# The end of a down-projection: gain rows fetched one stage earlier, factors by square root and reciprocal, the third row tile finished ahead of the fourth

## The chip, the cores and the metric

One core of one Trainium2 chip runs the kernel. The metric is the device time of one execution in microseconds (us). Smaller is better. Engines: PE (TensorE, the matrix engine), DVE (VectorE), ACT (ScalarE), POOL (GpSimd) and SP (SyncE, which here only issues DMAs).

## The reference, cut to what matters

One layer of an encoder trunk over 512 tokens of width 2048: a token mixer, a cross-attention and a ConvFFN, each with a residual add, and one final RMSNorm. The change lies in the last product and that norm:

```python
def conv_ffn(h, w_up, conv_w, w_down):
    u = causal_dwconv(h @ w_up, conv_w)
    gate, up = u[..., :D_FF], u[..., D_FF:]
    return (jax.nn.silu(gate) * up) @ w_down
...
    x = x + conv_ffn(h, w_ffn_up[l], ffn_conv[l], w_ffn_down[l])
    return rmsnorm(x, final_norm)
```

`rmsnorm` divides each token's row by the root of its mean square plus 1e-6 and multiplies by a gain row of 2048 numbers. D_FF is 5632.

## The kernel before, in words

Float32 products are made of three products of rounded parts: an operand is split into a high and a low part (`hi` by a cast on ACT, `lo` by a subtraction on DVE), and PE adds hi·hi, lo·hi and hi·lo (lines 1214, 1215 and 1216, always in this order).

The down-projection follows a scheme with seven block products in place of eight. It is run as four stages, `ph` 0 to 3 in the code, each with 22 steps `k` (KD = 22). In stages 0 to 2 a step has two halves, `j` 0 and 1, with a weight piece of 128x1024 each, and 12 matmuls of 128x128x512 per half. Stage 3 has one half per step. The list `slots` holds all halves in order. The stationary operand is the hidden activation: `hid` (128x512, loaded from `hf_d` by `fac_load`, line 950, five steps ahead), split by `fac_split` (line 956) one step ahead into `hdh` (ACT, line 149) and `hdl` (DVE, line 150). In stage 3 one `hid` serves two steps. The moving operand is the weight piece: loaded into `wst` (SP, line 854), in half of the cases added to a stored block (DVE, line 1006), and split by `make`/`sum_parts` into `whi` (ACT, line 972) and `wlo` (DVE, line 975), two halves ahead. `whi`, `wlo` have three buffers each, `wst` five.

The order on PE, DVE, ACT and POOL is the order of the code (a manual schedule). The loop over the slots does for each: `fac_load`, `fac_split`, `make`, then one entry of the list `later`, then the matmuls (`rows`). The list `later` holds work that has no weight to wait for: each stage's end fills it, and one entry leaves it per slot from step 1 on.

All tiles of 128x512 outside PSUM come from one pool (line 73, 64 buffers, taken by `T`, line 96). A tile gets a buffer that is free, and where none is, its first writer waits for the last reader of the tile that had it. In stage 2 (the third) the following hold buffers from its first step to its last: `store` for the steps up to 17 (line 988, two tiles each, 36), and the quadruples `c12`, `p7`, `c11` and `u2` (16). What is left serves `hid`, `hdh` and `hdl`.

At the end of stage 2 the fifth product gives two of the four row tiles of tokens their final sums (`c11`, `c12`); stage 3 adds the seventh product to the other two (`p7`; `u2` is already complete). The norm is done in stage 3 through `later`: squares on ACT with row sums (line 1222), gain rows from memory to all partitions (four POOL DMAs, `gains`, line 1294), the factors of row tiles 0 and 1 (`factor`: row sum, mean, then `rsqrt`, line 227 on, as the exponential of a logarithm on ACT with one refinement on DVE), then `out_tile` (line 1231: DVE multiplies by factor and gain, SP stores), and the product of `u2` with its gain (line 1308). The last two steps of stage 3 are held back and run quarter by quarter (lines 1313 to 1315), so that the sums of `p7` (line 1316) start while PE still works; then one `factor` for row tiles 2 and 3, four `out_tile` and four scaled copies on ACT (line 1323), all stored by SP.

Of the kernel before, what the change touches and what calls it, by code (L numbers as in the profile page):

```python
# [9 lines left out]
F32 = mybir.dt.float32  # L10
F32R = mybir.dt.float32r
AF = mybir.ActivationFunctionType
ALU = mybir.AluOpType
AX = mybir.AxisListType

P = 128
S = 512
D = 2048
# [8 lines left out]
EPS = 1e-6  # L27
# [42 lines left out]
def trunk(ctx: ExitStack, tc: tile.TileContext, g):  # L70
    nc = tc.nc
# [3 lines left out]
    sp = ctx.enter_context(tc.tile_pool(name="sp", bufs=2))  # L75
# [16 lines left out]
    def nm(s):  # L92
        uid[0] += 1
        return f"{s}_{uid[0]}"

    def T(s, dt=F32):
        return tp.tile([P, S], dt, tag="t", name=nm(s))
# [30 lines left out]
    cst = cpool.tile([P, 4], F32, tag="cst", name="cst")  # L128
# [116 lines left out]
    def rstd(ps, ms):  # L245
        nc.vector.tensor_scalar(ms, ps, 1.0 / D, EPS, op0=ALU.mult, op1=ALU.add)
        return rsqrt(ms, ps, 1.0 / D, cst[:, 0:1])
# [144 lines left out]
    for step in range(2 * KT):  # L392

        i, q = ((0, 0), (1, 0), (0, 1), (1, 1))[step] if step < 4 else divmod(step, 2)
# [309 lines left out]
    for i in range(8):  # L704
        for t in (1, 2, 0):
# [5 lines left out]
            elif t == 2:  # L711
                nc.vector.tensor_tensor(cg, ps, cg, op=ALU.mult)
                y = T("ysc")
# [56 lines left out]
    for half in range(2):  # L770
        for gq in range(2):
# [15 lines left out]
            for tq in range(2):  # L787
                j = 2 * half + tq
# [61 lines left out]
    tt = nc.vector.tensor_tensor  # L850
# [50 lines left out]
    with tc.manual_schedule(engines={mybir.EngineType.PE}):  # L901
        for idx in range(KT):
            n = order2[idx]
# [26 lines left out]
    def US(t):  # L930
        return us[0].tile([P, 1024], F32, tag="us", name=nm(t))
# [15 lines left out]
    def fkey(ph, k):  # L947
        return (ph, k // 2 * 2) if ph == 3 else (ph, k)
# [137 lines left out]
    for i in range(NF):  # L1086
# [27 lines left out]
        if i:  # L1114
            s2 = US("s2")
            tt(s2, s1, a11, op=ALU.subtract)
        else:
            s2 = a11
# [56 lines left out]
    def conv_step(c, a=0):  # L1175
        if not a:
            cv = T("ucv")
            tail.append(cv)
            nc.scalar.activation(cv, tail[-2], AF.Identity, scale=col(c + 2))
            a = 1  # L1180
        nc.vector.scalar_tensor_tensor(tail[-1][:, a:], tail[-2][:, : S - a], col(c + 2 - a), tail[-1][:, a:], op0=ALU.mult, op1=ALU.add)

    def gated():
# [6 lines left out]
    later = [gate_sum, lambda: conv_step(C_FCONV + 3 * last_i), lambda: conv_step(C_FCONV + 3 * last_i, 2), gated, up_sum,  # L1190
             lambda: conv_step(C_FCONV + 3 * (NF + last_i)), lambda: conv_step(C_FCONV + 3 * (NF + last_i), 2),
             lambda: tt(tail[1], tail[1], tail[3], op=ALU.mult)]
# [11 lines left out]
    def rows(bs, w, xs, off, first, last, only=None):  # L1204
        hi, lo = w
        xh, xl = xs
        for b in range(4) if only is None else (only,):
            t, ns = b // 2, b % 2
            c = slice(off + t * P, off + (t + 1) * P)
            n = slice(ns * S, (ns + 1) * S)  # L1210
            mm3_(bs[b], xh[:, c], xl[:, c], hi[:, n], lo[:, n], first, last)
# [6 lines left out]
    def add_rest(dst, j, m):  # L1218
        nc.gpsimd.dma_start(dst, x2t_d[j, :, m * S : (m + 1) * S], accum_op=ALU.add)

    def square(dst, ss, m):
        nc.scalar.activation(PG("sq"), dst, AF.Square, accum_out=ss[:, m : m + 1])

    def factor(ss, s2):

        tot = sp.tile([P, 2], F32, tag="tot", name=nm("tot"))
        nc.vector.tensor_reduce(tot, ss.rearrange("p (j m) -> p j m", j=2), axis=AX.X, op=ALU.add)
        ms = sp.tile([P, 2], F32, tag="ms2", name=nm("ms2"))
        return rstd(tot, ms)

    def out_tile(src, j, m, r):
        o = T("o")
        nc.vector.scalar_tensor_tensor(o, src, r[:, j % 2 : j % 2 + 1], gain[m], op0=ALU.mult, op1=ALU.mult)
        nc.sync.dma_start(g["out"][j][:, m * S : (m + 1) * S], o)

    with tc.manual_schedule(engines={mybir.EngineType.Activation, mybir.EngineType.DVE, mybir.EngineType.Pool, mybir.EngineType.PE}):
        for i, (ph, k, j) in enumerate(slots):
            if k == 0 and j == 0:
                bs = [banks(q) for q in range(1 if ph == 3 else 2)]
            a = ph * KD + k  # L1240
            for dist, act in ((5, fac_load), (2 if ph == 3 else 1, fac_split)):
                if a + dist < 4 * KD:
                    act((a + dist) // KD, (a + dist) % KD)
            make(i + 2)
            if ph == 3 and k % 2 == 0:
                add_block()
            if later and k > 0:
                later.pop(0)()
            if ph == 3 and k == KD - 2:
                continue  # L1250
            if ph == 3 and k == KD - 1:
                break
            rows(bs[j], pieces.pop(i), fac[fkey(ph, k)], (k % 2 if ph == 3 else 1 - j if ph == 2 else j) * S2, k == 0, k == KD - 1)
            if k < KD - 1:
                continue
            if ph == 0 and j == 0:
                c12 = quad("c12")
                for c, b in zip(c12, bs[0]):
                    nc.scalar.copy(c, b)
            elif ph == 0:  # L1260
                p7 = quad("p7")
                for c, b in zip(p7, bs[1]):
                    nc.scalar.copy(c, b)
                for q in range(4):
                    later.append(lambda q=q: add_rest(c12[q], q // 2, 2 + q % 2))
            elif ph == 1 and j == 0:
                c11 = quad("c11")
                for c, b in zip(c11, bs[0]):
                    nc.scalar.copy(c, b)
            elif ph == 1:  # L1270
                u2 = quad("u2")
                for u, c, b in zip(u2, c11, bs[1]):
                    tt(u, c, b, op=ALU.add)
                for q in range(4):
                    later.append(lambda q=q: tt(c12[q], c12[q], u2[q], op=ALU.add))
                    later.append(lambda q=q: tt(p7[q], p7[q], u2[q], op=ALU.add))
                for q in range(4):
                    later.append(lambda q=q: add_rest(c11[q], q // 2, q % 2))
            elif ph == 2 and j == 0:
                for q in range(4):  # L1280
                    tt(c11[q], c11[q], bs[0][q], op=ALU.add)
            elif ph == 2:
                ss01 = sp.tile([P, 8], F32, tag="ss01", name="ss01")
                ss23 = sp.tile([P, 8], F32, tag="ss23", name="ss23")
                gain, r, p5 = [], [], bs[1]

                def with_p5(q):
                    tt(u2[q], p7[q], p5[q], op=ALU.add)
                    add_rest(u2[q], 2 + q // 2, 2 + q % 2)
                    add_rest(p7[q], 2 + q // 2, q % 2)  # L1290
                    tt(c12[q], c12[q], p5[q], op=ALU.add)
                    square(c11[q], ss01, q // 2 * 4 + q % 2)

                def gains():
                    for m in range(4):
                        gain.append(T("gain"))
                        nc.gpsimd.dma_start(gain[m], g["fin"][:, m * S : (m + 1) * S].broadcast_to([P, S]))

                for q in range(4):
                    later.append(lambda q=q: with_p5(q))  # L1300
                for q in range(4):
                    later.append(lambda q=q: square(c12[q], ss01, q // 2 * 4 + 2 + q % 2))
                later.append(gains)
                later.append(lambda: r.append(factor(ss01, "a")))
                for q in range(4):
                    later.append(lambda q=q: (out_tile(c11[q], q // 2, q % 2, r[0]), square(u2[q], ss23, q // 2 * 4 + 2 + q % 2)))
                for q in range(4):
                    later.append(lambda q=q: (out_tile(c12[q], q // 2, 2 + q % 2, r[0]), tt(u2[q], u2[q], gain[2 + q % 2], op=ALU.mult)))
        for run in later:
            run()  # L1310
        nc.scalar.activation(cst[:, 3:4], cst[:, 0:1], AF.Ln)
        n = len(slots)
        for q in range(4):
            for i in (n - 2, n - 1):
                rows(bs[0], pieces[i], fac[fkey(3, KD - 2)], (i - n + 2) * S2, False, i == n - 1, only=q)
            tt(p7[q], p7[q], bs[0][q], op=ALU.add)
            square(p7[q], ss23, q // 2 * 4 + q % 2)
        rb = factor(ss23, "b")
        for q in range(4):
            j, m = 2 + q // 2, q % 2  # L1320
            out_tile(p7[q], j, m, rb)
            o = T("o")
            nc.scalar.activation(o, u2[q], AF.Identity, scale=rb[:, q // 2 : q // 2 + 1])
            nc.sync.dma_start(g["out"][j][:, (2 + m) * S : (3 + m) * S], o)


# [55 lines left out]
```

## Time and profile before

| | |
|---|---|
| three timed runs | 2753.11, 2755.22 and 2755.49 us; median 2755.22 |
| profiled execution, span from its first to its last instruction | 2753.7 us |
| PE busy | 2721.7 us (99%) |
| DVE, ACT, POOL busy | 2099.9, 1426.7, 267.5 us |
| mean granted PE clock | 0.997 |
| DMA, mean | 174 GB/s |

The page gives the span of the profiled execution as its own time; the timed runs are others. A row of the timeline reads: start in us from the span's start, duration in us (of the whole group where several are merged, "x2"), engine, line, operation, written tile <- read tiles, shape; in brackets the idle time of the engine ahead of it and what ended that. "SPq" is a DMA issue of SP. A busy PE says little by itself, since matmuls overlap: 0.39 us is one matmul's time from start to end, and what counts is the distance between starts.

### The profile page before, as it was taken

The numbers are of one execution on the slowest core, as the hardware profiler recorded it, in microseconds if no ns is written. First come the engines' busy times: TensorE is split into PE (matmuls) and PEld (weight loads), VectorE is DVE, ScalarE is ACT, GpSimd is POOL, SyncE is SP. The second block draws the span as 40 slices with busy tenths as digits, with TensorE's granted clock in tenths as the row PEclk, the third lists the DMA queues.
The fourth block names the chain that finished last, engine by engine and source line by source line (L and its number), as shares of the span: only waits on it lengthen the run. The fifth ranks groups of instructions, "written<-read, shape, count | busy, mean of one in ns | idle before, by whom it ended". The sixth has DMA issues, their size and how long they took to land.

```text
span 2753.7 us, 38057 instructions
## 1 busy us (share of the span) xinstructions
PE 2721.7 (99%) x14045; PEld 2300.9 (84%) x14045; DVE 2099.9 (76%) x3335; ACT 1426.7 (52%) x2092; POOL 267.5 (10%) x258
## 2 busy tenths in 40 slices
PE   9999999999999999999999999999999999999997
PEld 8888878888788888888788888888888888888885
DVE  7777647878775324445679999999999999877877
ACT  6674644345443323324566655556565655455455
POOL 2120001012110000110020000000000000000201
PEclk9999999999999999999999999999999999999999
DMA  7786853333332234445566677766767676864976
GB/s 266 236 294 195 270 174 105 109 95 93 107 92 90 90 102 139 147 149 169 168 174 178 172 191 185 188 182 182 194 180 189 176 195 202 257 186 146 290 229 177
DMA packets 213931, 479.35 MB, mean 174 GB/s; under 512 B 26720, under 2 KB 94192, under 8 KB 213744
## 3 DMA queue, kind: packets, MB, share of 16 engines
q1 hardware_dynamic: 154688, 372.81, 41.8%
q0 software_dynamic: 20272, 62.94, 12.8%
q10 hardware_dynamic: 38784, 41.17, 4.3%
q8 instruction: 110, 1.80, 0.3%
q14 instruction: 77, 0.63, 0.1%
HBM read 424.13 MB, written 52.71 MB: 173 GB/s over the span
## 4 chain that ended last, share of the span: by engine, by line
PE 67%; DVE 2%; DMA 1%; issue 1%; ACT 0%; DVEq 0%; SPq 0%; ACTq 0%
PE px L169 11%; PE px L172 6%; PE pz L169 6%; PE psd L1216 4%; PE psd L1215 4%; PE psd L1214 4%; PE psx L155 3%; PE pssc L154 3%; PE psx L154 3%; PE psx L156 3%; PE pssc L156 3%; PE pssc L155 3%; PE pz L172 3%; PE py L169 3%; PE py L172 1%; PE pss L781 1%
## 5 line engine op out<-in xcount | busy, mean ns | idle before, releaser
L144 DVE TENSOR_TENSOR wlo<-wst,whi 128x1024 fp32r<-128x1024 f32 x316 | 392.8, 1244 | 283.2 <-ACT whi L143 281.3
L143 ACT CAST whi<-wst 128x1024 fp32r<-128x1024 f32 x316 | 331.7, 1050 | 513.4 <-PE pssc L155 134.9
L169 PE MATMUL px<-xo,whi 128*128 128x512 f32 x1408 | 354.9, 394 | 4.5 <-ACT gb L1121 1.9
L860 ACT CAST whi<-wst 128x1024 fp32r<-128x1024 f32 x177 | 186.0, 1051 | 217.2 <-PE pz L169 126.5
L169 PEld LDWEIGHTS px<-xo,whi 128*128 128x128 f32 x1408 | 254.2, 189 | 51.2 <-ACT gb L1121 2.1
L1216 PE MATMUL psd<-wlo,hdh 128*128 128x512 f32 x616 | 240.6, 391 | 5.2 <-DVE wlo L975 5.2
L1215 PE MATMUL psd<-whi,hdl 128*128 128x512 f32 x616 | 239.8, 389 | 0.9 <-DVE hdl L150 0.9
L1214 PE MATMUL psd<-whi,hdh 128*128 128x512 f32 x616 | 239.8, 389 | 0.1
L861 DVE TENSOR_TENSOR wlo<-wst,whi 128x1024 fp32r<-128x1024 f32 x177 | 215.0, 1215 | 1.7 <-ACT whi L860 1.7
L172 PEld LDWEIGHTS px<-xo,wlo 128*128 128x128 f32 x1408 | 192.4, 191 | 13.8
L172 PE MATMUL px<-xo,wlo 128*128 128x256 f32 x1408 | 196.5, 282 | 0.0
L169 PE MATMUL pz<-xo,whi 128*128 128x512 f32 x704 | 176.3, 392 | 0.0
L860 ACT CAST whi<-s 128x1024 fp32r<-128x1024 f32 x131 | 136.2, 1040 | 76.1 <-PE px L169 38.7
L972 ACT CAST whi<-wst 128x1024 fp32r<-128x1024 f32 x99 | 104.3, 1053 | 122.1 <-issue 60.5
L861 DVE TENSOR_TENSOR wlo<-s,whi 128x1024 fp32r<-128x1024 f32 x131 | 159.3, 1216 | 0.0
L154 PE MATMUL psq<-hh,whi 128*128 128x512 f32 x384 | 156.0, 406 | 0.0
L154 PE MATMUL pssc<-hh,whi 128*128 128x512 f32 x384 | 153.2, 399 | 0.0
L156 PE MATMUL psq<-hh,wlo 128*128 128x512 f32 x384 | 150.6, 392 | 0.0
L155 PE MATMUL psq<-hl,whi 128*128 128x512 f32 x384 | 150.3, 391 | 0.0
L156 PE MATMUL pssc<-hh,wlo 128*128 128x512 f32 x384 | 149.9, 390 | 0.0
L155 PE MATMUL pssc<-hl,whi 128*128 128x512 f32 x384 | 149.6, 390 | 0.0
L169 PEld LDWEIGHTS pz<-xo,whi 128*128 128x128 f32 x704 | 126.6, 189 | 22.6
(362 smaller groups left out, 5924.5 us busy)
## 6 DMA issues: line engine op xcount, KB each, us to landing
wst<-in_w_up SPq DMA_DIRECT2D x132, 512.0 KB, 3.9
wst<-in_w_dn SPq DMA_DIRECT2D x121, 512.0 KB, 4.5
wst<-in_w_mix SPq DMA_DIRECT2D x112, 512.0 KB, 3.5
s<-in_w_up POOLq DMA_DIRECT2D x87, 512.0 KB, 6.1
s<-in_w_up SPq DMA_DIRECT2D x43, 512.0 KB, 4.4
hid<-hf_d SPq DMA_DIRECT2D x77, 256.0 KB, 5.3
wst<-in_w_xq SPq DMA_DIRECT2D x32, 512.0 KB, 5.1
wst<-in_w_xv SPq DMA_DIRECT2D x32, 512.0 KB, 3.6
```

The lines of the kernel that those rows point to most:

```text
L143: nc.scalar.copy(hi, st)
L144: nc.vector.tensor_tensor(lo, st, f(hi), op=ALU.subtract)
L154: nc.tensor.matmul(ps, wh, xh, start=first, stop=False)
L155: nc.tensor.matmul(ps, wh, xl, start=False, stop=False)
L156: nc.tensor.matmul(ps, wl, xh, start=False, stop=last)
L169: nc.tensor.matmul(ps, hi[:, k * P : (k + 1) * P], x, start=first and k == 0, stop=False, skip_group_check=True)
L172: nc.tensor.matmul(ps[:, n:], lo[:, k * P : (k + 1) * P], x[:, :n], start=False, stop=end, skip_group_check=True)
L860: nc.scalar.copy(hi, t)
L861: nc.vector.tensor_tensor(lo, t, f(hi), op=ALU.subtract)
L1214: nc.tensor.matmul(ps, xh, wh, start=first, stop=False)
L1215: nc.tensor.matmul(ps, xl, wh, start=False, stop=False)
L1216: nc.tensor.matmul(ps, xh, wl, start=False, stop=last)
```

## The change

Four things change. The gain rows are fetched by an entry of `later` that the end of stage 1 adds, so in stage 2, behind the thirteenth slot of it, and not in stage 3. `factor` takes the square root on ACT and the reciprocal on DVE, with the same refinement, and the early load of the logarithm's table is gone. Row tiles 2 and 3 get separate factors: row tile 2 is summed, scaled and stored while row tile 3's sums follow. The last two scaled copies are stored through ACT's own DMA queue. (As `later` in stage 3 is one entry shorter, each entry behind the gains leaves it one slot sooner.)

```diff
-    def factor(ss, s2):
+    def total(ss, n):
 
-        tot = sp.tile([P, 2], F32, tag="tot", name=nm("tot"))
-        nc.vector.tensor_reduce(tot, ss.rearrange("p (j m) -> p j m", j=2), axis=AX.X, op=ALU.add)
-        ms = sp.tile([P, 2], F32, tag="ms2", name=nm("ms2"))
-        return rstd(tot, ms)
+        tot, ms, y = (sp.tile([P, n], F32, tag=f"fa{n}{s2}", name=nm(s2)) for s2 in ("tot", "ms2", "fy"))
+        nc.vector.tensor_reduce(tot, ss.rearrange("p (j m) -> p j m", j=n), axis=AX.X, op=ALU.add)
+        nc.scalar.activation(y, tot, AF.Sqrt, scale=1.0 / D, bias=cst[:, 0:1])
+        nc.vector.tensor_scalar(ms, tot, 1.0 / D, EPS, op0=ALU.mult, op1=ALU.add)
+        return ms, y
+
+    def refined(ms, y):
+
+        t = sp.tile([P, ms.shape[1]], F32, tag=f"fa{ms.shape[1]}ft", name=nm("ft"))
+        nc.vector.reciprocal(y, y)
+        nc.vector.tensor_tensor(t, y, y, op=ALU.mult)
+        nc.vector.scalar_tensor_tensor(t, t, -0.5, ms, op0=ALU.mult, op1=ALU.mult)
+        nc.vector.scalar_tensor_tensor(y, t, 1.5, y, op0=ALU.add, op1=ALU.mult)
+        return y
+
+    def factor(ss, n):
+
+        return refined(*total(ss, n))
...
                 for q in range(4):
                     later.append(lambda q=q: add_rest(c11[q], q // 2, q % 2))
+                gain = []
+
+                def gains():
+                    for m in range(4):
+                        gain.append(T("gain"))
+                        nc.gpsimd.dma_start(gain[m], g["fin"][:, m * S : (m + 1) * S].broadcast_to([P, S]))
+
+                later.append(gains)
...
-                later.append(gains)
-                later.append(lambda: r.append(factor(ss01, "a")))
+                later.append(lambda: r.append(factor(ss01, 2)))
...
-        nc.scalar.activation(cst[:, 3:4], cst[:, 0:1], AF.Ln)
...
-            tt(p7[q], p7[q], bs[0][q], op=ALU.add)
-            square(p7[q], ss23, q // 2 * 4 + q % 2)
-        rb = factor(ss23, "b")
-        for q in range(4):
-            j, m = 2 + q // 2, q % 2
-            out_tile(p7[q], j, m, rb)
-            o = T("o")
-            nc.scalar.activation(o, u2[q], AF.Identity, scale=rb[:, q // 2 : q // 2 + 1])
-            nc.sync.dma_start(g["out"][j][:, (2 + m) * S : (3 + m) * S], o)
...
+        def last_scaled(q, r, queue):
+            o = T("o")
+            nc.scalar.activation(o, u2[q], AF.Identity, scale=r)
+            queue.dma_start(g["out"][2 + q // 2][:, (2 + q % 2) * S : (3 + q % 2) * S], o)
+
+        for q in range(4):
+            last_rows(q)
+        for q in range(2):
+            last_sum(q)
+            square(p7[q], ss23, q)
+        half = total(ss23[:, 0:4], 1)
+        last_sum(2)
+        square(p7[2], ss23, 4)
+        ra = refined(*half)
+        out_tile(p7[0], 2, 0, ra)
+        last_sum(3)
+        for q in range(2):
+            last_scaled(q, ra, nc.sync)
+        square(p7[3], ss23, 5)
+        out_tile(p7[1], 2, 1, ra)
+        rb = factor(ss23[:, 4:8], 1)
+        for q in (2, 3):
+            out_tile(p7[q], 3, q % 2, rb)
+            last_scaled(q, rb, nc.scalar)
```

Where instructions stand now, at three places. First DVE in stage 2, the steps 9 and 10, with what each row waits for (PE_49 is the count of matmuls done, Activation_49 that of ACT, DMAHW those of SP's DMAs). Before:

```order
L150 TENSOR_TENSOR hdl_23542<-hid_23353,hdh_23541 128x512 [waits DMAHW2_49,Activation_49]
L1006 TENSOR_TENSOR wst_23545<-wst_23545,store_21493 128x512 [waits DMAHW4_49]
L1006 TENSOR_TENSOR wst_23545<-wst_23545,store_21494 128x512
L975 TENSOR_TENSOR wlo_23550<-wst_23521,whi_23549 128x1024 [waits DMAHW3_49,PE_49,Activation_49]
L975 TENSOR_TENSOR wlo_23568<-wst_23545,whi_23567 128x1024 [waits PE_49,Activation_49]
L150 TENSOR_TENSOR hdl_23586<-hid_23401,hdh_23585 128x512 [waits DMAHW5_49,Activation_49]
```

Now:

```order
L150 TENSOR_TENSOR hdl_23550<-hid_23353,hdh_23549 128x512 [waits DMAHW2_49,PE_49,Activation_49]
L1006 TENSOR_TENSOR wst_23553<-wst_23553,store_21493 128x512 [waits DMAHW4_49]
L1006 TENSOR_TENSOR wst_23553<-wst_23553,store_21494 128x512
L975 TENSOR_TENSOR wlo_23558<-wst_23529,whi_23557 128x1024 [waits DMAHW3_49,Activation_49]
L975 TENSOR_TENSOR wlo_23576<-wst_23553,whi_23575 128x1024 [waits Activation_49]
L150 TENSOR_TENSOR hdl_23594<-hid_23401,hdh_23593 128x512 [waits DMAHW5_49,PE_49,Activation_49]
```

The order is the same; `hdl` has PE among its waits, which `wlo` behind it no longer needs. This holds for each `hdl` of the steps 9 to 18 of stage 2, and the count waited for is that of the last matmul of line 1215 of the step before (for step 10: the last one that reads `hdl` of step 9). Step 19 has no such wait, and 20 and 21 wait for matmuls of two steps before.

Second POOL's DMA issues in stage 2 and at their end in stage 3 (`store` is a block of the weights added to a stored one, `gain` a gain row). Before:

```order
L1024 DMA store_21234<-in_w_dn 128x512
L1024 DMA store_21235<-in_w_dn 128x512
L1024 DMA store_21340<-in_w_dn 128x512
L1024 DMA store_21341<-in_w_dn 128x512
...
L1024 DMA store_22019<-in_w_dn 128x512 x2
L1297 DMA gain_24415<-in_fin 128x512
L1297 DMA gain_24417<-in_fin 128x512
L1297 DMA gain_24419<-in_fin 128x512
L1297 DMA gain_24421<-in_fin 128x512
```

Now:

```order
L1024 DMA store_21234<-in_w_dn 128x512
L1024 DMA store_21235<-in_w_dn 128x512
L1298 DMA gain_23509<-in_fin 128x512
L1298 DMA gain_23511<-in_fin 128x512
L1298 DMA gain_23513<-in_fin 128x512
L1298 DMA gain_23515<-in_fin 128x512
L1024 DMA store_21340<-in_w_dn 128x512
L1024 DMA store_21341<-in_w_dn 128x512
```

The four gain DMAs moved from the end of POOL's queue to a place ahead of the additions to `store` of stage 2.

Third DVE at the end of the program (`p` is `p7`, `o` an output tile, `rsy` and `fy` a factor). Before:

```order
L1316 TENSOR_TENSOR p_3930_22159<-p_3930_22159,psd_24165 128x512
L1316 TENSOR_TENSOR p_3931_22160<-p_3931_22160,psd_24166 128x512
L1227 TENSOR_REDUCE tot_24735<-ss_24162 128x2
L246 TENSOR_SCALAR ms_4442_24737<-tot_24735 128x2
L240 TENSOR_TENSOR rst_24742<-rsy_24739 128x2
L241 SCALAR_TENSOR_TENSOR rst_24742<-rst_24742,ms_4442_24737 128x2
L242 SCALAR_TENSOR_TENSOR rsy_24739<-rst_24742,rsy_24739 128x2
L1233 SCALAR_TENSOR_TENSOR o_24746<-p_3928_22157,rsy_24739,gain_24415 128x512
L1233 SCALAR_TENSOR_TENSOR o_24752<-p_3929_22158,rsy_24739,gain_24417 128x512
```

Now:

```order
L1227 TENSOR_REDUCE tot_24728<-ss_24170 128x1
L1229 TENSOR_SCALAR ms_4440_24729<-tot_24728 128x1
L1334 TENSOR_TENSOR p_3930_22159<-p_3930_22159,psd_24173 128x512
L1235 RECIPROCAL fy_24730<-fy_24730 128x1
L1236 TENSOR_TENSOR ft_24737<-fy_24730 128x1
L1237 SCALAR_TENSOR_TENSOR ft_24737<-ft_24737,ms_4440_24729 128x1
L1238 SCALAR_TENSOR_TENSOR fy_24730<-ft_24737,fy_24730 128x1
L1247 SCALAR_TENSOR_TENSOR o_24742<-p_3928_22157,fy_24730,gain_23509 128x512
L1334 TENSOR_TENSOR p_3931_22160<-p_3931_22160,psd_24174 128x512
L1247 SCALAR_TENSOR_TENSOR o_24754<-p_3929_22158,fy_24730,gain_23511 128x512
L1227 TENSOR_REDUCE tot_24757<-ss_24170 128x1
L1229 TENSOR_SCALAR ms_4450_24758<-tot_24757 128x1
```

The sums of the third and fourth quarter now stand behind the reduction and behind the first factor and output tile of row tile 2.

More of the change, by code (lines that the diff above doesn't have):

```diff
@@ L1222, in square @@
         nc.scalar.activation(PG("sq"), dst, AF.Square, accum_out=ss[:, m : m + 1])
-    def factor(ss, s2):
-        tot = sp.tile([P, 2], F32, tag="tot", name=nm("tot"))
-        nc.vector.tensor_reduce(tot, ss.rearrange("p (j m) -> p j m", j=2), axis=AX.X, op=ALU.add)
-        ms = sp.tile([P, 2], F32, tag="ms2", name=nm("ms2"))
-        return rstd(tot, ms)
+    def total(ss, n):
[13 more added lines that the diff above has]
+        return refined(*total(ss, n))
     def out_tile(src, j, m, r):
         o = T("o")
-        nc.vector.scalar_tensor_tensor(o, src, r[:, j % 2 : j % 2 + 1], gain[m], op0=ALU.mult, op1=ALU.mult)
+        nc.vector.scalar_tensor_tensor(o, src, r, gain[m], op0=ALU.mult, op1=ALU.mult)
         nc.sync.dma_start(g["out"][j][:, m * S : (m + 1) * S], o)
@@ L1284, in trunk @@
                 ss23 = sp.tile([P, 8], F32, tag="ss23", name="ss23")
-                gain, r, p5 = [], [], bs[1]
+                r, p5 = [], bs[1]
                 def with_p5(q):
@@ L1292, in with_p5 @@
                     square(c11[q], ss01, q // 2 * 4 + q % 2)
[L1294 to L1297, printed above, removed]
                 for q in range(4):
@@ L1302, in trunk @@
                     later.append(lambda q=q: square(c12[q], ss01, q // 2 * 4 + 2 + q % 2))
-                later.append(gains)
-                later.append(lambda: r.append(factor(ss01, "a")))
+                later.append(lambda: r.append(factor(ss01, 2)))
                 for q in range(4):
-                    later.append(lambda q=q: (out_tile(c11[q], q // 2, q % 2, r[0]), square(u2[q], ss23, q // 2 * 4 + 2 + q % 2)))
+                    later.append(lambda q=q: (out_tile(c11[q], q // 2, q % 2, r[0][:, q // 2 : q // 2 + 1]), square(u2[q], ss23, q // 2 * 4 + 2 + q % 2)))
@@ L1307, in trunk, with last_rows @@
                 for q in range(4):
-                    later.append(lambda q=q: (out_tile(c12[q], q // 2, 2 + q % 2, r[0]), tt(u2[q], u2[q], gain[2 + q % 2], op=ALU.mult)))
+                    later.append(lambda q=q: (out_tile(c12[q], q // 2, 2 + q % 2, r[0][:, q // 2 : q // 2 + 1]), tt(u2[q], u2[q], gain[2 + q % 2], op=ALU.mult)))
         for run in later:
             run()
-        nc.scalar.activation(cst[:, 3:4], cst[:, 0:1], AF.Ln)
         n = len(slots)
-        for q in range(4):
+        def last_rows(q):
@@ L1314, in trunk, with last_sum @@
             for i in (n - 2, n - 1):
                 rows(bs[0], pieces[i], fac[fkey(3, KD - 2)], (i - n + 2) * S2, False, i == n - 1, only=q)
+        def last_sum(q):
             tt(p7[q], p7[q], bs[0][q], op=ALU.add)
-            square(p7[q], ss23, q // 2 * 4 + q % 2)
-        rb = factor(ss23, "b")
+        def last_scaled(q, r, queue):
+            o = T("o")
+            nc.scalar.activation(o, u2[q], AF.Identity, scale=r)
+            queue.dma_start(g["out"][2 + q // 2][:, (2 + q % 2) * S : (3 + q % 2) * S], o)
```

## The prediction

> **What bounds the kernel now.** I read the page's busy times first, then a table of windows over the last 140 us, then the timelines of DVE, PE, ACT and SP at the places that the change touches. The page:
>
> ```profile
> PE 2721.7 (99%) x14045; PEld 2300.9 (84%) x14045; DVE 2099.9 (76%) x3335; ACT 1426.7 (52%) x2092; POOL 267.5 (10%) x258
> PEclk9999999999999999999999999999999999999999
> ```
>
> PE is busy for 99% of the span, at the full granted clock. An edit can only gain in the few places where PE waits, or behind its last product; it can lose anywhere. The windows (length, then busy time of PE, weight load, DVE, ACT, POOL, then clock, DMA share, GB/s) show where PE waits:
>
> ```profile
> 2600.00:2640.00 40.00, 40.00 (x178) 33.14 (x177) 30.74 (x37) 19.75 (x23) 5.24 (x6) 1.00 0.98 310
> 2640.00:2670.00 30.00, 30.00 (x134) 24.84 (x133) 23.64 (x31) 14.28 (x17) 0.00 (x0) 1.00 0.71 223
> 2710.00:2720.00 10.00, 7.82 (x34) 5.87 (x32) 8.62 (x14) 4.57 (x11) 0.00 (x0) 1.00 0.63 219
> 2720.00:2730.00 10.00, 9.66 (x42) 7.32 (x41) 10.00 (x16) 4.80 (x8) 0.00 (x0) 1.00 0.25 90
> 2730.00:2740.00 10.00, 7.57 (x31) 5.41 (x30) 7.82 (x12) 4.15 (x8) 0.00 (x0) 1.00 0.14 52
> ```
>
> The first two rows lie in stage 2: PE never stops, DVE has a fifth of its time free. The last three lie in stage 3: PE loses time there, and DVE is the busier engine.
>
> **The change part by part.** I begin with the part that decides, the gain rows fetched in stage 2. They take four buffers of the tile pool from the thirteenth slot of stage 2 on. There, 36 buffers hold `store`, 16 the quadruples; of 64 that leaves 12, and with the gain rows 8. Each step keeps five `hid` in flight, and `hdh` and `hdl` of the step on PE: seven. The next `hdh` takes the eighth, so the next `hdl` gets the buffer of the present one, and must wait for the last matmul of line 1215 that reads it, the last but one of the step. The order of DVE, quoted above, shows this wait for ten steps (9 to 18); from then on `hid` is loaded half as often, and a buffer is free.
>
> Queued behind `hdl` on DVE are, for the next step, two additions and both `wlo`; behind the additions ACT's second `whi`; behind these SP's next weight loads and POOL's additions to `store`. PE needs `hdl` for the second product of the step and `wlo` for the third. The rows of DVE for one such chain, and of PE for its pace and for how it follows:
>
> ```profile
> 2661.84 0.69 DVE L150 TENSOR_TENSOR hdl<-hid,hdh 128x512 fp32r<-128x512 f32 x1
> 2662.45 1.29 DVE L1006 TENSOR_TENSOR wst<-wst,store 128x512 f32<-128x512 f32 x2
> 2663.65 1.22 DVE L975 TENSOR_TENSOR wlo<-wst,whi 128x1024 fp32r<-128x1024 f32 x1
> ...
> 2667.28 0.68 DVE L150 TENSOR_TENSOR hdl<-hid,hdh 128x512 fp32r<-128x512 f32 x1
> ```
>
> ```profile
> 2707.67 0.39 PE L1215 MATMUL psd<-whi,hdl 128*128 128x512 f32 x1
> ...
> 2711.53 0.39 PE L1214 MATMUL psd<-whi,hdh 128*128 128x512 f32 x1
> 2712.79 0.50 PE L1215 MATMUL psd<-whi,hdl 128*128 128x512 f32 x1 [0.87 <-DVE hdl L150]
> 2714.59 0.50 PE L1216 MATMUL psd<-wlo,hdh 128*128 128x512 f32 x1 [1.30 <-DVE wlo L975]
> 2714.93 0.39 PE L1214 MATMUL psd<-whi,hdh 128*128 128x512 f32 x1
> ...
> 2740.05 0.39 PE L1216 MATMUL psd<-wlo,hdh 128*128 128x512 f32 x1
> ```
>
> ```profile
> 2712.05 0.68 DVE L150 TENSOR_TENSOR hdl<-hid,hdh 128x512 fp32r<-128x512 f32 x1
> ...
> 2740.47 0.69 DVE L1316 TENSOR_TENSOR p<-p,psd 128x512 f32<-128x512 f32 x1 [0.67 <-PE psd L1216]
> ```
>
> From 2707.67 to 2711.53 are 17 products, so the pitch is 3.86/17 = 0.227 us, and a step of 24 takes 5.45, which is also the distance of the two `hdl` (2667.28 − 2661.84 = 5.44). Call e the end of the matmul waited for. DVE starts on a result of PE about 0.03 after its end (2740.05 + 0.39 = 2740.44; DVE at 2740.47). From the start of `hdl` to the end of the first `wlo` are 2663.65 + 1.22 − 2661.84 = 3.03. PE follows DVE by about 0.06 (2712.05 + 0.68 = 2712.73; PE at 2712.79). So the third product of the next step starts at e + 3.12. Without the wait it would start four pitches after the product that is waited for, at e − 0.39 + 0.91 = e + 0.52. That is a loss of 2.60. After a pause the next product follows by 0.34 in place of 0.227 (2714.59 to 2714.93), which adds 0.11: 2.71 for each step.
>
> The trace of before has one pause of the same form, hung on the same chain: from 2711.53 to 2714.93 three products take 3.40 where three pitches are 0.68, a loss of 2.72. Ten such steps cost 27.1. The bounds of one are 2.5 (if DVE is released one pitch ahead of the modelled end of the matmul) and 3.0 (if PE pays its slow restart twice, for `hdl` and for `wlo`, and 0.50 in place of 0.39 for one of them). DVE cannot make it up ahead: the chain starts only with e, and the next e is a whole step behind.
>
> The Trainium skill ("Perfetto Trace Analysis", "Optimization Strategy") has a rule that speaks against this edit: the same gap repeating on the engine that should be saturated can mean that there is no room for the next tile. Before shows no such gap in stage 2 (PE 40.00 of 40.00); by that rule the changed kernel would show ten.
>
> What the early fetch takes away lies in stage 3, together with the new factor. DVE's rows with the waits, and ACT's beside them:
>
> ```profile
> 2704.74 0.17 DVE L246 TENSOR_SCALAR ms<-tot 128x2 f32<-128x2 f32 x1
> 2706.58 0.16 DVE L240 TENSOR_TENSOR rst<-rsy 128x2 f32<-128x2 f32 x1 [1.68 <-ACT rsy L238]
> ...
> 2707.52 1.23 DVE L975 TENSOR_TENSOR wlo<-wst,whi 128x1024 fp32r<-128x1024 f32 x1 [0.39 <-ACT whi L972]
> ...
> 2711.38 0.75 DVE L1233 SCALAR_TENSOR_TENSOR o<-c,rsy,gain 128x512 f32<-128x512 f32 x1 [2.63 <-DMA gain<-in_fin]
> ```
>
> ```profile
> 2704.74 0.30 ACT L237 ACTIVATE rsy<-tot,cst 128x2 f32<-128x2 f32 x1 [1.51 <-DVE tot L1227]
> 2705.05 1.28 ACT L238 ACT_TABLE_LOAD   x1
> ```
>
> DVE waits 1.68 for the exponential, behind a table load of 1.28, then 0.39 for a `whi` that ACT made late, and 2.63 for the gain rows. With the square root (one ACT operation, as the 0.30 here) DVE waits about 0.16 (2705.04 against 2704.91) if the table stands; the reciprocal adds one small operation, 0.19 with its gap. DVE is the limit here, so 4.70 − 0.16 + 0.19, that is 4.3 of 4.70, should come back. Bounds: 2.6, if only the gain wait goes and a table load stays in the way, and 5.5; not more, since all stops of PE in the stage are 7.0 (from 2711.53 to 2740.05 95 pitches, 21.5, take 28.52), and the first, at 2712.79 and 2714.59, is 2.7 of these.
>
> Behind the last product (2740.44) 13.3 us follow until the span's end at 2753.7. The output tiles on DVE, ACT's work, two of SP's issues, and the time that issues of that line take to land:
>
> ```profile
> 2744.57 2.74 DVE L1233 SCALAR_TENSOR_TENSOR o<-p,rsy,gain 128x512 f32<-128x512 f32 x4
> ```
>
> ```profile
> 2742.46 1.28 ACT L238 ACT_TABLE_LOAD   x1
> ...
> 2744.57 2.56 ACT L1323 ACTIVATE o<-u,rsy 128x512 f32<-128x512 f32 x4 [0.62 <-DVE rsy L242]
> ```
>
> ```profile
> 2745.32 0.33 SPq L1324 DMA_DIRECT2D out_x<-o  x1
> ...
> 2749.18 0.60 SPq L1324 DMA_DIRECT2D out_x<-o  x1
> ```
>
> ```profile
> DMA to landing us min/median/max: 2.2/3.3/3.4
> ```
>
> Before, the factor is ready 4.1 after the last product, eight tiles follow, and SP's eight issues end at 2749.78. Now the table load is gone from that path, but the last sum stands behind the reduction, factor and output tile of row tile 2 and starts about 1.3 later, so the factor of row tile 3 is again ready at about 4.1. Then only two tiles on DVE and two on ACT remain (0.69 and 0.64 each, by the rows of four), with two queues: the last issue starts near 4.1 + 2 × 0.64 + 0.5 = 5.9 in place of 8.74. That is 2.8; with a last landing of 2.2 in place of 3.4, 4.0. I take 3.6, nearer to the second, since the queue before it is shorter.
>
> Then the edits that I cost at nothing: the gain DMAs now stand ahead of twelve additions to `store` in POOL's queue, which are needed only in stage 3. The final weight, its issue, its first reader, and the landing times of that line:
>
> ```profile
> 2701.65 0.34 SPq L854 DMA_DIRECT2D wst<-in_w_dn  x1
> ```
>
> ```profile
> 2730.87 1.28 DVE L1006 TENSOR_TENSOR wst<-wst,store 128x512 f32<-128x512 f32 x2
> ```
>
> ```profile
> DMA to landing us min/median/max: 3.4/6.2/12.4
> ```
>
> The last weight load is issued 29 us ahead of its use, and the slowest landing of the line in the last 210 us took 12.4: sooner buys nothing, and later by 10 would cost nothing.
>
> The sum, on this execution's own span: 2753.7 + 27.1 − 4.3 − 3.6 = 2772.9. The median of the timed runs is 1.5 above that span, so the forecast is 2755.22 + 19.2 = 2774.4.
>
> **The rivals.** First, the other side: the waits stand in the order but do not bite, because `hdl` is let go early enough. That needs the release 2.6 us or more ahead of the end of the step's last product but one, while the reader waited for is that very one. If another buffer is free on the chip all the same (the `hid` of the step gone sooner than the order says), only the gains remain: 2755.2 − 7.9 = 2747.3. It decides from a DVE chain shorter than 0.5 us, against 3.03 in the rows. I give it 0.05.
>
> Second, the clock: PE stops for over 2 us in every step, and its granted clock might fall behind each stop. If the 12 products behind each one ran at half rate, that is 10 × 12 × 0.227 = 27 more: 2801.6. Against it stands the window from 2710 to 2720, clock 1.00 through idle times of 0.87 and 1.30. The Trainium skill ("TensorE: Matmul & The Clock Gate", "Part 1: The HAM clock gate") has the rate halved after an idle window of about 3.4 us; the stops here would be shorter than that, so by that rule the clock stays. Chance 0.03.
>
> Third, the loads: `hid`'s DMA waits for buffers freed later, and SP's weight loads queue behind it. The group of weight loads from 2560 to 2668:
>
> ```profile
> wst<-in_w_dn SPq DMA_DIRECT2D x40, 512.0 KB, 6.3
> ```
>
> A load lands 6.3 after its issue here, at a DMA share of up to 0.98. If the additions had to wait one us more for it in each of the ten steps, the time would be 2784. Against it: slower steps of 8.2 also load the queues less, and five `hid` are in flight. Chance 0.04. That nothing changes at all would need gain and loss to cancel: 7.9 of gain is three stops, not ten; 0.01 with all such mixtures.
>
> **How the numbers follow.** The forecast has 0.87. Its own bounds: ten stops of 2.5 to 3.0 are 25 to 30; the gains 2.6 + 2.8 = 5.4 to 5.5 + 4.0 = 9.5. So +15.5 to +24.6, 2770.7 to 2779.8; one stop more or less that is only half covered widens it to 2769 to 2782. Outside lie the first rival, the second and the third, 0.12 together, so I do not stretch it to them. About 0.2% (5.5 us) is what a measurement of this kernel can tell from no change. Faster by more than that: 0.05; within it: 0.01; slower: 0.94.
>
> **What would show it right or wrong.** In the changed kernel's timeline of DVE, ten `hdl` in stage 2 should start 0.03 behind a PE matmul, one each 8.2 us, and PE should show a pair of stops in each, at `hdl` and at `wlo`, of about 0.3 and 1.8 us; PE's busy share in these 82 us should be about three quarters. In stage 3 the waits of 1.68 and 2.63 should be gone, and the last product should lie about 9.7 from the end. It is wrong if stage 2 shows no stops (first rival), if the clock there is below 1.00 (second), or if DVE's additions wait for `wst` (third).

## The result, and the profile after

The changed kernel takes 2790.06 us (median of 4 runs, 2788.57 to 2790.73), the kernel before 2755.35 beside it. The ratio is 1.0122, 95% interval 1.0111 to 1.0134: slower by 34.7 us, where 19.2 were forecast. The profiled execution spans 2786.8 us, 33.1 more than that of before. The page, its first row and the granted clock:

```profile
PE 2737.7 (98%) x14045; PEld 2306.7 (83%) x14045; DVE 2102.5 (75%) x3343; ACT 1422.2 (51%) x2087; POOL 267.7 (10%) x258
PEclk9999999999999999999999999999999999999999
```

The page hides it: forty slices of 70 us are too coarse for the clock. Two windows in stage 2 show it (columns as before):

```profile
2600.00:2640.00 40.00, 30.17 (x108) 21.77 (x106) 18.81 (x23) 10.07 (x12) 3.49 (x4) 0.91 0.77 211
2640.00:2660.00 20.00, 15.25 (x48) 11.12 (x48) 8.81 (x12) 5.05 (x7) 1.75 (x2) 0.83 0.61 165
```

PE, busy without a break from 2600 to 2670 us before, is now busy for three quarters of the time there, and the granted clock is 0.83 to 0.91. What PE waited for from 2560 us on (total, times, longest):

```profile
PE psd L1216 <- DVE wlo L975: 21.0, 14, 1.8
PE psd L1215 <- DVE hdl L150: 4.2, 10, 0.7
```

Ten stops at `hdl`, as the order said. (Of the fourteen waits for `wlo` ten belong to these stops; the other four are shorter than 0.9 us and lie elsewhere.) The timeline of DVE has the waits on PE in them:

```profile
2601.99 0.69 DVE L150 TENSOR_TENSOR hdl<-hid,hdh 128x512 fp32r<-128x512 f32 x1 [5.86 <-PE psd L1215]
...
2610.23 0.69 DVE L150 TENSOR_TENSOR hdl<-hid,hdh 128x512 fp32r<-128x512 f32 x1 [3.88 <-PE psd L1215]
...
2620.10 0.69 DVE L150 TENSOR_TENSOR hdl<-hid,hdh 128x512 fp32r<-128x512 f32 x1 [5.50 <-PE psd L1215]
...
2628.39 0.69 DVE L150 TENSOR_TENSOR hdl<-hid,hdh 128x512 fp32r<-128x512 f32 x1 [3.93 <-PE psd L1215]
```

The distances are 8.24, 9.87 and 8.29 us: two kinds of steps. PE's timeline shows the difference, one stop of each kind:

```profile
2620.85 0.50 PE L1215 MATMUL psd<-whi,hdl 128*128 128x512 f32 x1 [0.38 <-DVE hdl L150]
2623.19 0.50 PE L1216 MATMUL psd<-wlo,hdh 128*128 128x512 f32 x1 [1.84 <-DVE wlo L975]
2623.53 0.40 PE L1214 MATMUL psd<-whi,hdh 128*128 128x512 f32 x1
...
2631.48 0.67 PE L1216 MATMUL psd<-wlo,hdh 128*128 128x512 f32 x1 [1.84 <-DVE wlo L975]
2631.95 0.63 PE L1214 MATMUL psd<-whi,hdh 128*128 128x512 f32 x1
2632.37 0.63 PE L1215 MATMUL psd<-whi,hdl 128*128 128x512 f32 x1
...
2634.93 0.46 PE L1215 MATMUL psd<-whi,hdl 128*128 128x512 f32 x1
2635.23 0.39 PE L1216 MATMUL psd<-wlo,hdh 128*128 128x512 f32 x1
```

Both have the same pauses (0.4 and 1.84). Behind the first, products follow at full pace; behind the second for 3.45 us at 0.43 in place of 0.227, that is eight products at half rate, 1.6 us more. Such stretches begin behind seven of the ten stops.

Which stops bring the clock down looks like chance, but the trace shows what goes with it. The clock's records have the seven stretches begin at 2614.58, 2631.65, 2641.89, 2652.13, 2662.37, 2679.43 and 2689.68 us. Each lasts 3.41 us, and the distances between the beginnings are 10.24 or 17.07 us, three or five times 3.413. So in this trace the clock changes only at the edges of a fixed grid of 3.413 us. These are the grid windows with the two stops just shown, each with the window behind it (columns as before):

```profile
2621.41:2624.82 3.41, 1.63 (x7) 1.35 (x8) 2.95 (x3) 2.52 (x3) 0.00 (x0) 1.00 0.43 111
2624.82:2628.24 3.42, 3.42 (x17) 2.81 (x16) 0.00 (x0) 0.00 (x0) 0.00 (x0) 1.00 0.74 265
...
2628.24:2631.65 3.41, 1.17 (x5) 0.43 (x4) 3.15 (x5) 1.19 (x2) 1.67 (x2) 1.00 0.36 88
2631.65:2635.06 3.41, 3.41 (x9) 2.63 (x10) 1.11 (x1) 1.32 (x2) 0.08 (x1) 0.50 0.83 136
```

An edge of the grid cuts the first stop, and its window holds 1.78 us without a product (3.41 − 1.63); the clock stays. The second stop lies in one window whole, 2.24 us, and the next window runs at half rate. The ten traces of this document hold 26 such falls ahead of the last product. In 25 of them the window ahead has 1.83 us or more without a product; of the almost 8000 other windows two reach 1.83 (1.83 and 1.84). One fall, in the experiment with three products in the pause, follows a window with 1.52 and stays unexplained. This bound was read off the finished traces; no run was made to try it.

The account by stages needs common points: the sums of `u2` at the beginning of stage 2, those of `c11` behind the first half of its last step, and the last product. Before:

```profile
2551.89 2.48 DVE L1273 TENSOR_TENSOR u<-c,psd 128x512 f32<-128x512 f32 x4
...
2670.29 2.47 DVE L1281 TENSOR_TENSOR c<-c,psd 128x512 f32<-128x512 f32 x4
```

Now:

```profile
2551.62 2.48 DVE L1287 TENSOR_TENSOR u<-c,psd 128x512 f32<-128x512 f32 x4
...
2709.96 2.47 DVE L1303 TENSOR_TENSOR c<-c,psd 128x512 f32<-128x512 f32 x4
```

```profile
2776.21 0.39 PE L1216 MATMUL psd<-wlo,hdh 128*128 128x512 f32 x1
```

| | before | changed | difference | forecast |
|---|---|---|---|---|
| up to stage 2 | 2551.89 | 2551.62 | −0.3 | |
| stage 2 | 118.40 | 158.34 | +39.9 | +27.1 |
| from there to the end of the last product | 70.15 | 66.64 | −3.5 | −4.3 |
| from there to the end | 13.3 | 10.2 | −3.1 | −3.6 |

Stage 2 is ten stops of 8.24 − 5.44 = 2.80 us, 28.0, and seven stretches at half rate of 9.87 − 8.24 = 1.63 us, 11.4: 39.4 of the 39.9. (The tenth stop is 0.35 longer than the others: PE waits 0.74 for `hdl` there in place of 0.39.)

### The profile page after: what moved, and what is told of

Its sections match the earlier page's. It is cut to its first block, busy times and chain, and to the rows that moved or that the text cites. A ratio compares the mean times of both kernels' runs of the same rounds, so it can differ in the third digit from the quotient of the medians.

```text
span 2786.8 us, 38075 instructions
## 1 busy us (share of the span) xinstructions
PE 2737.7 (98%) x14045; PEld 2306.7 (83%) x14045; DVE 2102.5 (75%) x3343; ACT 1422.2 (51%) x2087; POOL 267.7 (10%) x258
## 4 chain that ended last, share of the span: by engine, by line
PE 65%; DVE 3%; DMA 1%; issue 1%; ACT 1%; ACTq 0%; DVEq 0%; SPq 0%
PE px L169 11%; PE px L172 6%; PE pz L169 6%; PE psd L1216 4%; PE psd L1215 4%; PE psd L1214 4%; PE pssc L154 3%; PE pssc L156 3%; PE pssc L155 3%; PE pz L172 3%; PE psx L155 3%; PE psx L154 3%; PE psx L156 3%; PE py L169 3%; PE py L172 1%; PE pss L781 1%
## 5 line engine op out<-in xcount | busy, mean ns | idle before, releaser
L1216 PE MATMUL psd<-wlo,hdh 128*128 128x512 f32 x616 | 246.3, 400 | 21.3 <-DVE wlo L975 21.0
L1215 PE MATMUL psd<-whi,hdl 128*128 128x512 f32 x616 | 245.6, 399 | 4.2 <-DVE hdl L150 4.2
L1216 PEld LDWEIGHTS psd<-wlo,hdh 128*128 128x128 f32 x616 | 118.4, 192 | 52.6 <-DVE wlo L975 28.0
```

What stands on the lines that cost most here:

```text
L1215: nc.tensor.matmul(ps, xl, wh, start=False, stop=False)
L1216: nc.tensor.matmul(ps, xh, wl, start=False, stop=last)
```

## The experiments

My theory after the result: the four buffers of the gain rows make all ten stops, and PE's idle time in a stop, if long enough, brings its clock down. Against it: that the early gain DMAs do harm by themselves (traffic, POOL's queue), that the other parts of the change have a share, or that the low clock has a cause of its own.

### e1_gain_late: the gain rows back in stage 3, the rest of the change kept

```diff
-                later.append(gains)        # end of stage 1
+                later.append(gains)        # end of stage 2, ahead of factor
                 later.append(lambda: r.append(factor(ss01, 2)))
```

> The changed kernel with one part undone: the gain rows are fetched in stage 3 again, the rest of the change stays. If the lack of buffers makes the ten stops (theory), stage 2 runs without a stop at a granted clock of 1.00, and what is left is the gain of the tail (3.1 us by the traces: 13.3 to 10.2 from the last product to the end) and of the square root in stage 3 (1 to 2 us, as the wait for the gain rows is back): 2750.5, 0.9982 of before. If the new factor or the new end had a share in the 40 us that stage 2 lost (rival), the time stays above 2755.

Measured: 2751.11 us, ratio 0.9985 (0.9976 to 0.9994). The loss is gone, so the new factor and the new end have no share in it. Stage 3 shows what became of the waits (DVE):

```profile
2702.36 0.17 DVE L1235 RECIPROCAL fy<-fy 128x2 f32<-128x2 f32 x1 [0.16 <-ACT fy L1228]
...
2708.48 0.75 DVE L1247 SCALAR_TENSOR_TENSOR o<-c,fy,gain 128x512 f32<-128x512 f32 x1 [3.95 <-DMA gain<-in_fin]
```

The wait for the exponential is down from 1.68 to 0.16, and the wait for the gain rows has grown from 2.63 to 3.95: without the early fetch, the new factor for the most part moves the wait. The pause of PE that follows is, but for 0.2, the one that the prediction quoted of before:

```profile
2709.89 0.50 PE L1215 MATMUL psd<-whi,hdl 128*128 128x512 f32 x1 [0.68 <-DVE hdl L150]
2711.70 0.80 PE L1216 MATMUL psd<-wlo,hdh 128*128 128x512 f32 x1 [1.30 <-DVE wlo L975]
2712.29 0.63 PE L1214 MATMUL psd<-whi,hdh 128*128 128x512 f32 x1
```

Here the half rate follows it, there it did not. The grid windows with the pauses, first of before (its grid follows from the stretch at half rate that begins at 2744.25, behind the last product), then of this run, show the difference:

```profile
2710.12:2713.53 3.41, 2.30 (x9) 1.32 (x8) 2.15 (x4) 0.17 (x2) 0.00 (x0) 1.00 0.80 317
2713.53:2716.95 3.42, 2.36 (x10) 1.98 (x11) 3.42 (x6) 2.94 (x6) 0.00 (x0) 1.00 0.45 135
```

```profile
2708.15:2711.56 3.41, 1.56 (x6) 0.74 (x4) 3.08 (x6) 0.36 (x1) 0.00 (x0) 1.00 0.83 290
2711.56:2714.98 3.42, 3.29 (x8) 2.61 (x9) 3.42 (x6) 3.42 (x8) 0.00 (x0) 0.50 0.38 137
```

Before, an edge parts the pauses into 1.11 and 1.06 us; here 1.85 us come together in one window.

### e2_gain_early: the kernel before, with the early gain rows alone

```diff
+                later.append(gains)        # end of stage 1
...
-                later.append(gains)        # end of stage 2
                 later.append(lambda: r.append(factor(ss01, "a")))
```

> The kernel before with that one part alone: the gain rows are fetched in stage 2. Theory: all of the loss comes from here, +39.9 in stage 2 as in the changed kernel, less up to 2.6 for the wait for the gain rows in stage 3: 2792 (2791 to 2795), ten pairs of stops, granted clock 0.8 to 0.9 there. Rival, that the loss needs the other parts too: below 2775.

Measured: 2790.23 us, ratio 1.0126 (1.0112 to 1.0140), 2 below the forecast and just below its range. From 2530 us on PE waits for

```profile
PE psd L1216 <- DVE wlo L975: 21.5, 16, 1.8
PE psd L1215 <- DVE hdl L150: 4.3, 10, 0.7
```

Ten stops again, and seven stretches at half rate. This one part, alone, makes the whole loss. From the sums of `c11` to the end of the last product it takes 67.3 us in place of 70.15, so it also brings most of the gain in stage 3.

### e3_hid4: the changed kernel with one buffer more

```diff
-            for dist, act in ((5, fac_load), (2 if ph == 3 else 1, fac_split)):
+            for dist, act in ((4, fac_load), (4 if ph == 2 and k < KD - 4 else 5, fac_load), (2 if ph == 3 else 1, fac_split)):
```

> The whole changed kernel, but in the steps 0 to 17 of stage 2 the hidden activation is loaded four steps ahead in place of five, so that one more buffer is free and each hdl waits for a matmul of two steps before. The gain DMAs stay early, and POOL's queue as it is. Theory (the buffer makes the stops, the stops make the low clock): no stop in stage 2, clock 1.00, time 2755.3 - 3.5 - 3.1 = 2748.7. Rival (the early gain DMAs themselves, their traffic or POOL's queue): the stops stay, about 2790. A third case, loads four ahead come too late: DVE or ACT waits for hid, 2755 or more.

Measured: 2748.71 us, ratio 0.9973 (0.9964 to 0.9982). The windows over the same part of stage 2:

```profile
2600.00:2640.00 40.00, 39.94 (x176) 32.67 (x176) 31.23 (x37) 18.85 (x22) 5.24 (x6) 1.00 1.03 323
2640.00:2680.00 40.00, 40.00 (x178) 33.11 (x177) 33.61 (x44) 18.55 (x23) 0.19 (x1) 1.00 0.65 205
```

None of the ten stops, full clock. The gain DMAs are as early as in the changed kernel and POOL's queue is the same; so neither does harm, and the lack of one buffer is the cause. This has the lowest median of all versions, and hidden activations loaded four steps ahead come in time.

### e4_three_stops: the gain rows at step 14

```diff
-                later.append(gains)
...
+            if (ph, k, j) == (2, 14, 0):
+                gains()
```

> The changed kernel with the gain rows fetched at step 14 of stage 2, so that only the hdl of steps 16, 17 and 18 waits for the step before. Theory: three stops of 2.8, 2748.7 + 8.4 = 2757 if the clock stays at 1.00, and up to 1.6 more for each stop behind which it falls: 2757 to 2762. If the clock falls only after a long row of stops: 2757. Rival (the loss is not counted in stops): 2775 or more.

Measured: 2761.43 us (2757.32 to 2764.84, 10 runs), ratio 1.0020 (1.0011 to 1.0029). Over the version without stops that is 12.7 us for three stops: 8.4 by the price of a stop, which leaves 4.3, the price of two or three stretches at half rate. The windows around the three:

```profile
2644.00:2652.00 8.00, 6.08 (x19) 4.27 (x18) 2.76 (x4) 0.70 (x1) 0.00 (x0) 0.81 0.81 244
2652.00:2660.00 8.00, 6.01 (x24) 4.43 (x24) 4.02 (x6) 2.29 (x4) 0.00 (x0) 1.00 0.44 132
2660.00:2668.00 8.00, 7.45 (x26) 6.00 (x27) 5.97 (x8) 3.83 (x6) 0.00 (x0) 0.79 0.71 229
```

The clock falls behind the first and the third stop and not behind the second. One stop is enough; it takes no long row of them. The grid windows of the three hold 1.84, 1.84 and 2.22 us without a product: the first and the second lie at the bound, one on each side.

### e5_fill7 and e6_fill3: something to do for PE in the pause

Work is added that changes no result: products with a tile of zeros, seven or three in each of the ten pauses.

```diff
         nc.tensor.matmul(ps, xl, wh, start=False, stop=False)
+        for _ in range(fill):
+            nc.tensor.matmul(ps, zero, wh, start=False, stop=False)
         nc.tensor.matmul(ps, xh, wl, start=False, stop=last)
```

> The whole changed kernel, with work added: in the steps 9 to 18 of stage 2, seven more products per step with a tile of zeros as the stationary operand stand on PE between the second and the third product, where it waits 1.84 for wlo. They add zero to the bank, and at 0.227 each take 1.6 of these 1.84. DVE's chain is the same, so each stop still costs 2.8. If the low granted clock comes from PE's idle time (theory), the clock is 1.00 in stage 2 and the time 2790.1 - 7 x 1.6 = 2778.9. If it has another cause (rival), seven or so steps still run at half rate, and the time is 2790 or more.

> The same with three such products in place of seven: about 1.1 of the 1.84 stays idle, and the 0.39 ahead of it. If any stop of a microsecond brings the clock down, 2790 as in the changed kernel; if the clock needs the longer idle time, 2779 as with seven; some steps slow, between.

Measured: 2778.65 us with seven (ratio 1.0085, 1.0069 to 1.0100), 2778.37 with three (1.0084, 1.0070 to 1.0098). One stop with seven, and a window:

```profile
2620.43 0.50 PE L1217 MATMUL psd<-whi,hdl 128*128 128x512 f32 x1 [0.39 <-DVE hdl L152]
2620.77 1.78 PE L1219 MATMUL psd<-whi,zero 128*128 128x512 f32 x7
2622.78 0.50 PE L1220 MATMUL psd<-wlo,hdh 128*128 128x512 f32 x1 [0.22 <-DVE wlo L977]
```

```profile
2620.00:2640.00 20.00, 18.16 (x74) 13.41 (x74) 11.92 (x15) 6.80 (x9) 1.75 (x2) 1.00 0.67 196
```

The stop is as long as before, the pause is filled, the clock stays at 1.00, and the kernel with 70 more products is 11.4 us faster: the idle time of PE is what brings the clock down. With three, a pause of 1.13 is left, and one stretch of ten runs at half rate:

```profile
2629.45 0.50 PE L1220 MATMUL psd<-wlo,hdh 128*128 128x512 f32 x1 [1.14 <-DVE wlo L977]
...
2637.70 0.60 PE L1220 MATMUL psd<-wlo,hdh 128*128 128x512 f32 x1 [1.13 <-DVE wlo L977]
```

Behind the first of these it does not fall, behind the second it does. So falls become rarer as the pause is filled: seven of ten at 1.84, one at 1.13, none at 0.22, each with 0.4 ahead. In these steps a grid window holds at most 1.53 us without a product with three, and at most 0.61 with seven. The one fall, behind a window with 1.52, is the exception named above.

### e7_wlo_first: a shorter chain on DVE

```diff
         prepare(i)
-        prepare(i + 1)
+        turn = i < len(slots) and slots[i][0] == 2 and slots[i][2] == 0
+        if not turn:
+            prepare(i + 1)
         if i < len(slots) and i not in pieces:
             pieces[i] = sum_parts(sums.pop(i))
+        if turn:
+            prepare(i + 1)
```

> The changed kernel, with DVE's order altered in stage 2: the wlo of a step's first half stands ahead of the two additions for its second half. If the chain on DVE sets the price of a stop (theory), PE waits about 0.4 for hdl, 0.6 for the first wlo and 0.7 for the second, a loss of 2.3 in place of 2.8 for each step, 5 less in all; with no pause over a microsecond the clock stays at 1.00, 11.3 less: 2774. If the clock follows the sum of the idle time and not the single pause, 2785. Rival (the price doesn't hang on this chain): 2790.

Measured: 2777.92 us, ratio 1.0083 (1.0069 to 1.0097), 4 above the forecast. PE in one step, and the window around it:

```profile
2619.64 0.50 PE L1219 MATMUL psd<-whi,hdl 128*128 128x512 f32 x1 [0.39 <-DVE hdl L150]
2620.77 0.50 PE L1220 MATMUL psd<-wlo,hdh 128*128 128x512 f32 x1 [0.63 <-DVE wlo L975]
...
2624.45 0.50 PE L1220 MATMUL psd<-wlo,hdh 128*128 128x512 f32 x1 [0.53 <-DVE wlo L975]
...
2627.65 0.50 PE L1219 MATMUL psd<-whi,hdl 128*128 128x512 f32 x1 [0.40 <-DVE hdl L150]
```

```profile
2620.00:2640.00 20.00, 16.23 (x61) 10.63 (x60) 11.23 (x14) 6.91 (x9) 1.75 (x2) 1.00 0.74 205
```

The pauses came nearly as worked out (0.4, 0.6, and 0.5 in place of 0.7), and the clock stays at 1.00, though PE is idle for almost a fifth of these 20 us: it does not follow the sum over a step. No grid window in these steps holds more than 1.03 us without a product. That a single long pause is needed is not shown by this: in the first experiment two pauses, neither over 1.3, made up the 1.85. But a step takes 8.01 us (2619.64 to 2627.65), 2.56 more than without a stop and not 2.3; I had counted PE's slow restart for two of the three pauses. With that, 2.4 of the 12.1 us gained come from the shorter chain, and the other 9.7 are near the 11.4 that the clock cost.

### e8_sqrt_only: the kernel before with the new factor alone

```diff
-        nc.scalar.activation(y, ps, AF.Ln, scale=scale, bias=bias)
-        nc.scalar.activation(y, y, AF.Exp, scale=-0.5)
+        nc.scalar.activation(y, tot, AF.Sqrt, scale=1.0 / D, bias=cst[:, 0:1])
...
+        nc.vector.reciprocal(y, y)
```

> The kernel before with the new factor alone (square root and reciprocal; one factor for row tiles 2 and 3 as before, no early table load, gain rows in stage 3). In stage 3 the wait of 1.68 for the exponential goes, but the gain rows land when they did, so the wait for them grows by as much: nothing. At the end, from the sum's reduction to the first output tile 1.3 (the changed kernel's second factor) in place of 2.6: 2755.4 - 1.3 = 2754.1. If the wait in stage 3 counts by itself, 2752.5.

Measured: 2753.65 us, ratio 0.9997 (0.9988 to 1.0006): not to be told from no change. The profile shows the parts:

```profile
2709.88 0.75 DVE L1247 SCALAR_TENSOR_TENSOR o<-c,fy,gain 128x512 f32<-128x512 f32 x1 [3.82 <-DMA gain<-in_fin]
```

```profile
2738.52 0.39 PE L1216 MATMUL psd<-wlo,hdh 128*128 128x512 f32 x1
```

In stage 3 the wait for the gain rows has taken the place of that for the exponential, as in the first experiment. From the end of the last product (2738.91) to the span's end (2750.9) are 12.0 us in place of 13.3.

## Why the prediction was wrong

**The ten stops**: right, in place, number, order of waits and almost in price. 2.80 us each in place of 2.71; DVE starts `hdl` on PE's release, and PE waits 0.4 for `hdl` and 1.84 for `wlo`. The first and the third experiment show that the buffer is the cause, the second that it is enough. The rule of the Trainium skill ("Perfetto Trace Analysis", "Optimization Strategy") that the same gap repeating can mean no room for the next tile agrees with it: ten gaps of 1.84.

**The clock**: this step failed. Its price was put at nothing on the strength of one row, "Against it stands the window from 2710 to 2720, clock 1.00 through idle times of 0.87 and 1.30", and the clock rival got 0.03. The clock fell behind seven of ten stops, for eight products each where the rival had reckoned twelve behind every one, and cost 11.4 us, most of the 15.5 that the forecast was short. The row could not carry the conclusion. Its two pauses fell into two windows of the grid, with 1.11 and 1.06 us idle, which was luck; nearly the same pauses in the first experiment, 0.68 and 1.30, put 1.85 us into one window and did bring the clock down. And each was shorter than the pause that I forecast myself, 1.8; so they could not speak for that one. I also left the rival's cost out of the range, as all or nothing, where a cost for a part of the stops was the likely form. The rule of the Trainium skill that I set beside it ("TensorE: Matmul & The Clock Gate", "Part 1: The HAM clock gate") has the rate fall after an idle window of about 3.4 us. The runs here differ: 1.83 to 2.53 us without a product in a window of 3.41 us were enough, seven times in ten stops. That a stretch at half rate lasts 3.41 us fits the length of the window that the rule names.

**The gains in stage 3**: 3.5 in place of 4.3. The mechanism held: with the early gain rows the wait of 2.63 is gone, that of 1.68 is down to 0.16, and the last product comes 3.5 sooner after stage 2. The first output tile of row tile 0 no longer waits for its gain row:

```profile
2746.30 0.75 DVE L1247 SCALAR_TENSOR_TENSOR o<-c,fy,gain 128x512 f32<-128x512 f32 x1
```

What I had not seen is that the two terms are not two. In the last experiment, the square root alone, the stage is 0.5 shorter; in the second, the early fetch alone, it is 2.9 shorter. The six traces with the whole of this code in stage 3 differ among themselves by 0.9, so neither the 0.5 nor what the square root adds to the early fetch (0.6 here) is clear of noise. Without the early fetch the wait for the gain rows takes up most of the 1.68. (The first experiment can't say it by its length: its stage 3 has a stretch at half rate.)

**The tail**: 3.1 in place of 3.6. The last issue came where it was forecast (ACT's queue, 5.84 behind the last product):

```profile
2782.44 0.36 ACTq L1339 DMA_DIRECT2D out_x<-o  x1
```

```profile
DMA to landing us min/median/max: 2.6/2.9/3.2
```

What was too small is the landing, for which I had taken 2.2. By the last experiment 1.3 of the 3.1 come from the new factor; the split of row tiles and the second queue are left with 1.8, which no run measured by itself.

**The edits costed at nothing** cost nothing that can be told: the third experiment has them all, and its 2748.7 is the sum of the gains (3.5 + 3.1, from 2755.4), which its interval bears out to about 2.5 us either way.

The rivals: that the waits do not bite was wrong. That loads come late was wrong too: no addition on DVE waited for `wst` in the ten steps, DVE waited for PE there.

## What to carry to other kernels

Before a tile is taken earlier from a shared pool, count what the pool's other users hold at that time: one buffer too few ties a prefetch to the step that is running, and everything queued behind it on that engine goes from parallel to serial. A stop of PE is to be priced twice, by its length and by the slow products that may follow it; here filling the pause, or splitting it into shorter ones that lie apart, saved the second price. A row in which a pause did no harm shows little until it is known where the pause lay on the grid. And a wait that ends just behind another one is worth only their union.

## What the runs showed of the hardware that was not expected

PE's granted clock fell to half (products 0.43 apart in place of 0.227) for 3.41 us at a time, behind pauses well under 2 us: behind seven of ten stops with a pause of 1.84, in each of two kernels, one of ten at 1.13, none of ten at 0.22 and none of ten with 0.63 and 0.53. The changes lie on a fixed grid of 3.413 us, and what went with a fall was the time without a product inside one window of it: 1.83 us or more in 25 of 26 falls. Among stops of the same length, the place on the grid went with the difference. Why one window with 1.52 brought the clock down while another with 1.53 in the same run did not is open, and no run moved a stop on the grid to try the bound.
